# Splitting the first stage of a decoder block into a scale-only pass and a shift pass

## The chip, the cores and the metric

The kernel runs on one core of a Trainium2 chip. The metric is the device time of one execution in microseconds (us), and the reported number is the median of several executions. A profile is one further execution with the hardware profiler on; its own time is given apart. The engines are named as the profile names them: PE (TensorE, matrix products), DVE (VectorE, elementwise), ACT (ScalarE, activations and casts), POOL (GpSimd) and SP (SyncE, which in this kernel issues every transfer, in order, from one queue).

## The reference: what is computed

One block of a decoder with 512 tokens and width 2048, in float32. The parts that matter here:

```python
mod = silu(c) @ w_ada + b_ada                 # six rows of 2048: sh1, sc1, gt1, sh2, sc2, gt2
h = rmsnorm(x, norm1_g) * (1 + sc1) + sh1
p = h @ w_in                                  # 3360 recurrence columns, 1024 pooling columns
y_rwkv = rwkv7(token_shift_mix(p[:, :3360]))  # 16 heads of 64, recurrence over the tokens
u = p[:, 3360:]
mean = causal window mean of u (windows 2, 4, 8, 16, one per group of 256 columns)
y_pool = ((mean - u) @ pool_w + pool_b) * pool_scale
x = x + gt1 * (concat(y_rwkv, y_pool) @ w_out)
h = rmsnorm(x, norm2_g) * (1 + sc2) + sh2
x = x + gt2 * (silu(gate) * val of conv3(h @ w_up)) @ w_down
out = rmsnorm(x, norm_f_g)
```

The pooling branch takes a window mean minus the token itself. The term that sh1 adds to u is the same for every token, and a constant minus its own mean is zero. So the pooling columns can be computed without sh1, and the per-token factor of the first RMS norm can be put on after the product with w_in instead of ahead of it.

## The kernel before, in words

Activations lie transposed: features on the 128 partitions, the 512 tokens along the free axis. A width of 2048 is 16 slabs, called k. Every large product is made of three float32r products of split operands (hi·hi, hi·lo, lo·hi): `mm3`, lines 115 to 118. A weight block of 128x512 comes in by one 256 KB transfer (`wraw`, 4 buffers), ACT casts it to its hi half (L110, `whi`, 3 buffers) and DVE subtracts to get the lo half (L112, `wlo`, 3 buffers).

**First stage** (lines 171 to 223). All of x (4 MB) is loaded first; ACT squares it, DVE sums the squares, PE adds over partitions and broadcasts the RMS factor `rs`. Then a loop over the 16 k. For each k two rows of the adaLN product are made on DVE (L209: a 128x2048 block `wa` of 1 MB is multiplied by silu(c) and summed along the free axis), one for the scale sc1 (j = 16 + k), one for the shift sh1 (j = k). DVE forms `gsc` (L211) and `mod` (L213), then `modulate` makes the normalised input (L144 on DVE, L145 on ACT for the hi half, L146 on DVE for the lo half), and 24 products add slab k into eight PSUM banks `pf`: the first eight column tiles of w_in. The hi and lo halves of all 16 slabs stay in the slots `ah` and `al` (list H) for the later column tiles.

**Mixer stage** (lines 226 to 694). Four groups g = 0 to 3 of four heads each go through `front` and `rest`: a long chain over PE, ACT and DVE with two round trips through DRAM (`dn` and `nl`, then `dxy` and `X`) and a recurrence over 8 chunks. These steps have high priority in the scheduler that sets each engine's order. Below them, the other column tiles of w_in (48 products each, PSUM tag `mm`) are spread between them: 6 tiles of r, k and v in each of the first three groups, spilled to DRAM and read back by the next group. In the last group the 8 pooling tiles stand there (lines 672 to 680), each copied by ACT and spilled to DRAM (`su`). Four calls of `pool` (lines 274 to 300) then load a pair of them (`upad`, in the same memory as the tile k of the recurrence), do 1 to 4 window additions and a subtraction on DVE, two small products, and write the result to `mixd`. `load_pw` takes its memory from the tag `war`, which has two buffers. The same two buffers serve `ada_rest` (L341, L342): 96 rows of the remaining adaLN product, 512 KB each, 24 per group in program order, multiplied and summed on DVE. Because tags are handed out in program order, the last 24 of these rows can start only when the last `pool` calls have given their `war` buffers back.

**After that** comes the output product (`out_block`: 8 banks, four passes over four slabs, so 96 products per pass), which needs `mixd` read back (`mxl`, in the memory of `wraw`), then the MLP. From there on PE has work without a break to the end.

Of the kernel before, what the change touches and what calls it, by code (L numbers as in the profile page):

```python
# [59 lines left out]
def block_kernel(ctx, tc, a, out, stop=None, dbg=None):  # L60
# [113 lines left out]
    if True:  # L174
# [10 lines left out]
        with tc.tile_pool(name="ps00", bufs=1, space=PSUM) as ps00:
            pst = ps00.tile([P, NC], F32, tag="st", name="pst")
            acc = p0.tile([P, T], F32, tag="sacc", name="sacc")
            for k in range(KT):
                if k == 0:
                    S.activation(acc, xs[k], AF.Square)  # L190
                    continue
# [1 line left out]
                S.activation(sq, xs[k], AF.Square)
                V.tensor_add(acc, acc, sq)
            rms_stats(pst, acc)
            psb = ps00.tile([P, T], F32, tag="bc", name="psb")
            rms_bcast(psb, rms_rows(p0, pst, NC), NC)
            S.copy(rstd, psb)
        ps0ctx = ExitStack()
        ps0 = ps0ctx.enter_context(tc.tile_pool(name="ps0", bufs=1, space=PSUM))  # L200
        pf = [ps0.tile([P, T], F32, tag=f"pf{i}", name=f"pf{i}") for i in range(8)]
        H = []
        for k in range(KT):
            for part in (1, 0):
                j = part * 16 + k
                wa = p0.tile([P, D], F32, tag="wa", name="wa", bufs=4)
                nc.sync.dma_start(wa, a["ada1"][j, :, :])
                jk = p0.tile([P, D], BF16, tag="jk", name="jk", bufs=1)
                V.scalar_tensor_tensor(jk, wa, 1.0, cb, op0=ALU.mult, op1=ALU.mult,  # L209
                                       accum_out=mod[:, j : j + 1])  # L210
            V.scalar_tensor_tensor(gsc1[:, k : k + 1], mod[:, 16 + k : 17 + k], b1p[:, k : k + 1],  # L211
                                   col("n1", k), op0=ALU.add, op1=ALU.mult)
# [805 lines left out]
```

## Time and profile before

| what | value |
|---|---|
| median of 3 runs | 2406.44 us (2405.72 to 2408.11) |
| the profiled execution | 2404.25 us, span 2402.5 us |
| last product of the first stage starts | 153.53 us |
| start of the scores of group 3 | 573.3 us |
| end of the recurrence chain of group 3 (L646) | 666 us |
| the last of the 96 adaLN rows (L342) | 790 us |

Times in the views are microseconds from the start of the span; means of one instruction are nanoseconds. In the views of stretches, each engine has its busy time and, in brackets, its number of instructions; the last three numbers are the granted PE clock, the mean busy share of the DMA engines, and GB/s. PE's busy time counts overlapping products in full, so a busy PE is not a PE at its peak; the distance from one start to the next is what says how fast it goes.

### The profile page before, as it was taken

How to read it: one execution, taken by the hardware profiler on the slowest of the kernel's cores; microseconds unless marked ns; L12 is line 12 of the kernel's file. 1: busy time of each engine (PE TensorE's matmuls, PEld its weight loads, DVE VectorE, ACT ScalarE, POOL GpSimd, SP SyncE). 2: the span in 40 equal slices, each digit the busy share in tenths (PEclk: the TensorE clock that was granted, in tenths of full speed). 3: DMA queues.
4: the chain of work that ended last, by engine and by line, in shares of the span. 5: the costliest groups of instructions: out<-in, count | busy, mean ns of one | idle time of the engine just before them, and what ended most of it. 6: DMA issues, size and time to landing. Idle time of an engine off the chain costs nothing.

```text
span 2402.5 us, 36790 instructions
## 1 busy us (share of the span) xinstructions
PE 2247.2 (94%) x14434; PEld 1819.8 (76%) x14434; DVE 1338.7 (56%) x2208; ACT 815.5 (34%) x1339; POOL 27.2 (1%) x30
## 2 busy tenths in 40 slices
PE   4778898999988999999999999999999999999997
PEld 3656575676666799887888888888888888888887
DVE  7987786646446558568344434444344434444457
ACT  3242242434332346432233322332233323323333
POOL 0000000000000003000000000000000000000000
PEclk9989999999999999999999999999999999999999
DMA  9966767423257646357323333223322332333335
GB/s 360 342 207 198 232 215 221 135 85 107 75 170 249 221 158 203 122 186 253 99 98 97 97 96 97 97 97 97 97 97 97 97 97 97 96 98 97 98 99 175
DMA packets 182896, 351.79 MB, mean 146 GB/s; under 512 B 35905, under 2 KB 42305, under 8 KB 178497
## 3 DMA queue, kind: packets, MB, share of 16 engines
q1 hardware_dynamic: 182722, 349.44, 45.7%
q8 instruction: 113, 1.85, 0.3%
q14 instruction: 61, 0.50, 0.1%
HBM read 333.63 MB, written 15.74 MB: 145 GB/s over the span
## 4 chain that ended last, share of the span: by engine, by line
PE 71%; DMA 12%; DVE 11%; issue 3%; ACT 2%; SPq 1%; DVEq 0%; POOL 0%; ACTq 0%; POOLq 0%
PE b L116 21%; PE b L118 21%; PE b L117 21%; DMA war<-ada 5%; DVE jk L209 3%; PE mm L118 2%; PE mm L116 2%; PE mm L117 2%; DVE war L342 1%; DVE wlo L112 1%; DMA slot<-ada 1%; DMA wraw<-wup 1%; DMA wraw<-win 1%; DMA upad<-su 1%; DMA dxy<-xyl 0%
## 5 line engine op out<-in xcount | busy, mean ns | idle before, releaser
L110 ACT CAST whi<-wraw 128x512 fp32r<-128x512 f32 x788 | 489.1, 622 | 1253.4 <-PE b L117 959.6
L112 DVE TENSOR_TENSOR wlo<-wraw,whi 128x512 fp32r<-128x512 f32 x772 | 533.3, 692 | 665.8 <-ACT whi L110 657.4
L118 PE MATMUL b<-hh,wlo 128*128 128x512 f32 (+1 forms) x1472 | 561.1, 381 | 5.5 <-DVE wlo L112 4.1
L116 PE MATMUL b<-hh,whi 128*128 128x512 f32 (+1 forms) x1472 | 560.2, 381 | 0.0
L117 PE MATMUL b<-hl,whi 128*128 128x512 f32 (+1 forms) x1472 | 559.5, 380 | 0.0
L116 PE MATMUL b<-ah,whi 128*128 128x512 f32 (+1 forms) x1120 | 405.2, 362 | 15.7 <-ACT whi L110 12.8
L118 PE MATMUL b<-ah,wlo 128*128 128x512 f32 (+1 forms) x1120 | 403.8, 361 | 0.8 <-DVE wlo L112 0.8
L117 PE MATMUL b<-al,whi 128*128 128x512 f32 (+1 forms) x1120 | 403.4, 360 | 0.0
L118 PEld LDWEIGHTS b<-hh,wlo 128*128 128x128 f32 x1472 | 277.1, 188 | 61.2 <-DVE wlo L112 7.3
L116 PEld LDWEIGHTS b<-hh,whi 128*128 128x128 f32 x1472 | 277.2, 188 | 53.0 <-ACT whi L110 0.5
L117 PEld LDWEIGHTS b<-hl,whi 128*128 128x128 f32 x1472 | 277.1, 188 | 52.5
L116 PEld LDWEIGHTS b<-ah,whi 128*128 128x128 f32 x1120 | 212.5, 190 | 51.6 <-ACT whi L110 14.3
L118 PEld LDWEIGHTS b<-ah,wlo 128*128 128x128 f32 x1120 | 212.6, 190 | 33.5 <-DVE wlo L112 2.5
L117 PEld LDWEIGHTS b<-al,whi 128*128 128x128 f32 x1120 | 212.6, 190 | 32.6 <-DVE al L139 1.0
L118 PE MATMUL mm<-ah,wlo 128*128 128x512 f32 x432 | 179.3, 415 | 3.9 <-DVE wlo L112 3.9
L116 PE MATMUL mm<-ah,whi 128*128 128x512 f32 x432 | 178.3, 413 | 1.7 <-ACT whi L110 1.7
L117 PE MATMUL mm<-al,whi 128*128 128x512 f32 x432 | 176.5, 409 | 0.4 <-issue 0.4
L342 DVE SCALAR_TENSOR_TENSOR war<-war,cq 128x1024 f32<-128x1024 f32 x96 | 117.1, 1223 | 70.1 <-DMA war<-ada 69.5
L880 DVE SCALAR_TENSOR_TENSOR x<-b,mod,x 128x512 f32<-128x512 f32 x80 | 59.7, 751 | 111.7 <-PE b L118 111.7
L118 PEld LDWEIGHTS mm<-ah,wlo 128*128 128x128 f32 x432 | 83.0, 192 | 27.9 <-DVE wlo L112 6.9
L116 PEld LDWEIGHTS mm<-ah,whi 128*128 128x128 f32 x432 | 83.3, 193 | 23.5 <-issue 4.3
L117 PEld LDWEIGHTS mm<-al,whi 128*128 128x128 f32 x432 | 83.2, 193 | 20.2 <-issue 3.1
(220 smaller groups left out, 1708.7 us busy)
## 6 DMA issues: line engine op xcount, KB each, us to landing
wraw<-wup SPq DMA_DIRECT2D x368, 256.0 KB, 3.0
war<-ada SPq DMA_DIRECT2D x96, 512.0 KB, 4.3
wraw<-wdn SPq DMA_DIRECT2D x192, 256.0 KB, 2.7
wraw<-win SPq DMA_DIRECT2D x140, 256.0 KB, 4.0
wa<-ada SPq DMA_DIRECT2D x32, 1024.0 KB, 6.3
wraw<-wout SPq DMA_DIRECT2D x88, 256.0 KB, 3.4
slot<-ada SPq DMA_DIRECT2D x64, 256.0 KB, 3.7
sp<-spill SPq DMA_DIRECT2D x18, 256.0 KB, 2.3
```

What stands on the lines that cost most here:

```text
L110: S.copy(hi[:, 0:w], raw[:, 0:w])
L112: eng.tensor_tensor(lo[:, 0:w], raw[:, 0:w], hi[:, 0:w].bitcast(F32), op=ALU.subtract)
L116: PE.matmul(ps, wh, xh, start=start, stop=False)
L117: PE.matmul(ps, wh, xl, start=False, stop=False)
L118: return PE.matmul(ps, wl, xh, start=False, stop=stop)
L209: V.scalar_tensor_tensor(jk, wa, 1.0, cb, op0=ALU.mult, op1=ALU.mult, accum_out=mod[:, j : j + 1])
L342: V.scalar_tensor_tensor(wa, wa, 1.0, cq[0], op0=ALU.mult, op1=ALU.mult, accum_out=modq[:, kq, j : j + 1])
L880: V.scalar_tensor_tensor(x2[f], ps, mod[:, 80 + f : 81 + f], x2[f], op0=ALU.mult, op1=ALU.add)
```

## The change

The first stage becomes two passes over the 16 slabs.

*First pass.* Slab by slab, x is loaded (no longer all at first), the scale row of the adaLN product is made, and the raw x is multiplied by `gsc` alone (hi on ACT, lo on DVE, into the slots `ah` and `al`). These are multiplied with seven of the eight pooling tiles, in seven PSUM banks (21 products per slab). The squares for the RMS factor are summed alongside. After the pass, the eighth bank serves for the RMS statistics and its broadcast, then for the eighth pooling tile, a full product of 48 with all 16 slabs. Each of the eight tiles is multiplied by `rs` on DVE and spilled to `su` (256 KB each, two buffers `us`).

*Second pass.* Slab by slab the shift row is made, the full normalised input is formed as before in the same slots, and the eight column tiles that were the first stage's before are computed in all eight banks.

The eight pooling tiles of the last group are gone from the mixer stage; `pool` reads `su` as it did. The input arrays on the host are laid out to fit (`winu`, `winu7`). Weights are read as often as before.

```diff
-        xs = []
-        for i in range(8):
-            xt = p0.tile([P, 2, T], F32, tag=f"x{i}", name=f"x{i}")
-            nc.sync.dma_start(xt, a["xT"][:, 2 * i : 2 * i + 2, :])
...
+        pu = [pf_bank(i) for i in range(7)]
+        xs, H1 = [], []
+        acc = p0.tile([P, T], F32, tag="sacc", name="sacc")
+        for k in range(KT):
+            if k % 2 == 0:
+                xt = p0.tile([P, 2, T], F32, tag=f"x{k // 2}", name=f"x{k // 2}")
+                nc.sync.dma_start(xt, a["xT"][:, k : k + 2, :])
+                xs += [xt[:, 0, :], xt[:, 1, :]]
+            ada_row(16 + k)
+            V.scalar_tensor_tensor(gsc1[:, k : k + 1], mod[:, 16 + k : 17 + k], b1p[:, k : k + 1],
+                                   col("n1", k), op0=ALU.add, op1=ALU.mult)
+            hi, lo = slots(k)
+            S.activation(hi, xs[k], AF.Copy, scale=gsc1[:, k : k + 1])
+            V.scalar_tensor_tensor(lo, xs[k], gsc1[:, k : k + 1], hi[:, :].bitcast(F32), op0=ALU.mult, op1=ALU.subtract)
+            H1.append((hi, lo))
+            feed(pu, a["winu"], k, H1[k])
...
+                S.activation(sq, xs[k], AF.Square)
+                V.tensor_add(acc, acc, sq)
+        pst = pf_bank(7)
+        rms_stats(pst, acc)
...
+        S.copy(rstd, psb)
+        pu.append(pf_bank(7))
+        project(pu[7], a["winu7"], H1)
+        for i in range(8):
+            t = p0.tile([P, T], F32, tag="us", name="us", bufs=2)
+            V.tensor_mul(t, pu[i], rstd)
+            d = tc.dram_tile([P, T], F32, name=f"su{i}")
+            nc.sync.dma_start(d, t)
+            su[POOLS[i // 2], i % 2] = d
+        pf = [pf_bank(i) for i in range(8)]
         H = []
         for k in range(KT):
-            for part in (1, 0):
-                j = part * 16 + k
...
+            ada_row(k)
             V.tensor_add(mod[:, k : k + 1], mod[:, k : k + 1], col("b_ada", k))
             h = p0.tile([P, T], F32, tag="h", name="h", bufs=2)
             hi, lo = slots(k)
             modulate(hi[:, :], lo[:, :], h, xs[k], rstd, gsc1[:, k : k + 1], mod[:, k : k + 1])
...
+            feed(pf, a["win0"], k, H[k])
...
-        else:
-            for n, gi in enumerate(POOLS):
-                for i in range(2):
-                    ps = win_tile(27 + 2 * n + i)
-                    t = ra.tile([P, T], F32, tag="spill", name="spill", bufs=2)
-                    S.copy(t, ps)
-                    d = tc.dram_tile([P, T], F32, name=f"su{gi}_{i}")
-                    nc.sync.dma_start(d, t)
-                    su[gi, i] = d
```

Three places in the order of the engines' instructions show what moves.

First stage, DVE, one slab. Names: `jk` is an adaLN row (L209 before, L191 after), `wlo` a weight's lo half, `sacc` the sum of squares, `al` the lo half of the input. Before, one slab of the loop:

```order
L209 SCALAR_TENSOR_TENSOR jk,mod<-wa,cb 128x2048
L211 SCALAR_TENSOR_TENSOR gsc_86<-mod,b1p,vec 128x1
L144 SCALAR_TENSOR_TENSOR h<-x_120,gsc_86,rs_132 128x512
L209 SCALAR_TENSOR_TENSOR jk,mod<-wa,cb 128x2048
L112 TENSOR_TENSOR wlo<-wraw,whi 128x512
L213 TENSOR_TENSOR mod<-mod,vec 128x1
L112 TENSOR_TENSOR wlo<-wraw,whi 128x512
L146 SCALAR_TENSOR_TENSOR al_431<-h,mod,ah_430 128x512
```

The change, two slabs of the first pass:

```order
L191 SCALAR_TENSOR_TENSOR jk,mod<-wa,cb 128x2048
L112 TENSOR_TENSOR wlo<-wraw,whi 128x512
L211 SCALAR_TENSOR_TENSOR gsc_86<-mod,b1p,vec 128x1
L112 TENSOR_TENSOR wlo<-wraw,whi 128x384
L223 TENSOR_TENSOR sacc<-sacc,sq 128x512
L215 SCALAR_TENSOR_TENSOR al_271<-x_218,gsc_86,ah_270 128x512
L223 TENSOR_TENSOR sacc<-sacc,sq 128x512
L191 SCALAR_TENSOR_TENSOR jk,mod<-wa,cb 128x2048
L112 TENSOR_TENSOR wlo<-wraw,whi 128x512
L211 SCALAR_TENSOR_TENSOR gsc_86<-mod,b1p,vec 128x1
L112 TENSOR_TENSOR wlo<-wraw,whi 128x384
L215 SCALAR_TENSOR_TENSOR al_318<-x_310,gsc_86,ah_317 128x512
```

A slab has one `jk` row instead of two, and the sum of squares has moved into the loop.

Group 3, DVE, from the two solve steps X and Y into the first chunks of the recurrence. Names: `sall` and `rc` belong to the recurrence, `sw` and `z` to `pool`, `war` is a row of `ada_rest`. Before (L555 X, L561 Y):

```order
L555 TENSOR_TENSOR X<-X,bt 128x1024
L284 TENSOR_TENSOR sw<-sw 128x2x513
L561 TENSOR_TENSOR Y<-Y,bt 128x1024
L289 SCALAR_TENSOR_TENSOR z<-sw,upad 128x1024
L547 TENSOR_TENSOR pm<-bt,mlev 128x1024
L290 TENSOR_TENSOR z<-sw,prec 128x2x16
L112 TENSOR_TENSOR wlo<-wraw,whi 128x512
L291 TENSOR_TENSOR z<-z,upad 128x2x16
L278 MEMSET upad 128x2x16
L561 TENSOR_TENSOR Y<-Y,bt 128x1024
L604 TENSOR_SCALAR sall<-ch,fdec 128x64 x2
L112 TENSOR_TENSOR wlo<-wraw,whi 128x512
```

The change (L580 X, L586 Y, L367 the adaLN row):

```order
L580 TENSOR_TENSOR X<-X,bt 128x1024
L367 SCALAR_TENSOR_TENSOR war,modq<-war,cq 128x1024
L586 TENSOR_TENSOR Y<-Y,bt 128x1024
L572 TENSOR_TENSOR pm<-bt,mlev 128x1024
L367 SCALAR_TENSOR_TENSOR war,modq<-war,cq 128x1024
L586 TENSOR_TENSOR Y<-Y,bt 128x1024
L367 SCALAR_TENSOR_TENSOR war,modq<-war,cq 128x1024
L629 TENSOR_SCALAR sall<-ch,fdec 128x64 x2
L605 TENSOR_TENSOR rc<-ch,xv 128x128
L367 SCALAR_TENSOR_TENSOR war,modq<-war,cq 128x1024
L627 SCALAR_TENSOR_TENSOR sall<-ch,fdec,sf 128x64 x2
L605 TENSOR_TENSOR rc<-ch,xv 128x128
```

All four `pool` calls now stand ahead of X, and the last 24 adaLN rows, which stood behind the whole chain, stand between its steps: 13 of them ahead of the sum that closes the recurrence (`y`, L648 after, L623 before), 18 ahead of its last step (L671 after, L646 before).

Group 3, SP, the same rows' transfers. Before:

```order
L299 DMA mixd_105<-mxp 128x512
L341 DMA war<-ada 128x1024
L299 DMA mixd_106<-mxp 128x512
L280 DMA upad<-su_1_5930 128x512
L341 DMA war<-ada 128x1024 x2
L299 DMA mixd_101<-mxp 128x512
```

The change (L366 the adaLN row, L324 a result of `pool`, L108 a weight block, L723 a read of `mixd`):

```order
L324 DMA mixd_105<-mxp 128x512
L366 DMA war<-ada 128x1024
L324 DMA mixd_106<-mxp 128x512
L366 DMA war<-ada 128x1024
L324 DMA mixd_101<-mxp 128x512
L366 DMA war<-ada 128x1024 x2
L324 DMA mixd_102<-mxp 128x512
L366 DMA war<-ada 128x1024 x19
L108 DMA wraw<-wout 128x512
L366 DMA war<-ada 128x1024
L723 DMA mxl<-mixd_97 128x512
```

No weight block stands between these rows any more; before, a weight block or a read of `mixd` stood behind nearly every one of them.

More of the change, by code (lines that the diff above doesn't have):

```diff
@@ L51 @@
     WIN_ORDER += [f"r{_p}", f"k{_p}", f"v{_p}"]
-WIN_ORDER += [f"u{2 * _g + _i}" for _g in POOLS for _i in range(2)]
+POOL_ORDER = [f"u{2 * _g + _i}" for _g in POOLS for _i in range(2)]
 MIX_ORDER = [0, 1, 2, 3, 4, 5] + [8 + 2 * _g + _i for _g in POOLS for _i in range(2)] + [6, 7]
@@ L178, in block_kernel @@
         nc.sync.dma_start(cact, cb[0:1, :])
-        xs = []
-        for i in range(8):
-            xt = p0.tile([P, 2, T], F32, tag=f"x{i}", name=f"x{i}")
-            nc.sync.dma_start(xt, a["xT"][:, 2 * i : 2 * i + 2, :])
-            xs += [xt[:, 0, :], xt[:, 1, :]]
-        rstd = p0.tile([P, T], F32, tag="rs0", name="rs0")
[L185 to L191, printed above, removed]
+        su = {}
@@ new lines, in block_kernel, with pf_bank, ada_row @@
+        rstd = p0.tile([P, T], F32, tag="rs0", name="rs0")
+        ps0ctx = ExitStack()
+        ps0 = ps0ctx.enter_context(tc.tile_pool(name="ps0", bufs=1, space=PSUM))
+        def pf_bank(i):
+            return ps0.tile([P, T], F32, tag=f"pf{i}", name=f"pf{i}")
+        def ada_row(j):
+            wa = p0.tile([P, D], F32, tag="wa", name="wa", bufs=4)
+            nc.sync.dma_start(wa, a["ada1"][j, :, :])
+            jk = p0.tile([P, D], BF16, tag="jk", name="jk", bufs=1)
+            V.scalar_tensor_tensor(jk, wa, 1.0, cb, op0=ALU.mult, op1=ALU.mult, accum_out=mod[:, j : j + 1])
@@ new lines, in feed @@
+        def feed(banks, src, k, hl):
+            n = len(banks)
+            for i0 in range(0, n, WC // P):
+                m = min(WC // P, n - i0)
+                wh, wl = split_weights(src[k, :, i0 * P : (i0 + m) * P])
+                for ii in range(m):
+                    sl = slice(ii * P, (ii + 1) * P)
+                    mm3(banks[i0 + ii], wh[:, sl], wl[:, sl], *hl, start=k == 0, stop=k == KT - 1)
+        pu = [pf_bank(i) for i in range(7)]
+        xs, H1 = [], []
+        acc = p0.tile([P, T], F32, tag="sacc", name="sacc")
@@ L194, in block_kernel @@
                 V.tensor_add(acc, acc, sq)
[L195 to L201, printed above, removed]
+        pst = pf_bank(7)
+        rms_stats(pst, acc)
+        dg = rms_rows(p0, pst, NC)
+        psb = pf_bank(7)
+        rms_bcast(psb, dg, NC)
+        S.copy(rstd, psb)
[8 more added lines that the diff above has]
+        pf = [pf_bank(i) for i in range(8)]
         H = []
         for k in range(KT):
-            for part in (1, 0):
-                j = part * 16 + k
[L206 to L212, printed above, removed]
+            ada_row(k)
             V.tensor_add(mod[:, k : k + 1], mod[:, k : k + 1], col("b_ada", k))
```

17 lines of the change are left out of this document (9 added, 8 removed).

## Prediction

> **What bounds the kernel now.** I read the page's slices first, then a table of stretches by stage, then the timeline inside the two stages that the change touches.
>
> ```profile
> PE   4778898999988999999999999999999999999997
> DVE  7987786646446558568344434444344434444457
> ...
> 154.00:301.00 147.00, 119.66 (x1527) 86.83 (x1528) 108.16 (x199) 52.05 (x88) 1.91 (x2) 0.93 0.66 207
> 301.00:448.00 147.00, 131.48 (x1574) 94.86 (x1573) 106.20 (x193) 52.49 (x87) 0.95 (x1) 0.95 0.65 207
> 448.00:552.00 104.00, 98.50 (x1467) 71.36 (x1466) 60.53 (x112) 43.12 (x73) 0.96 (x1) 1.00 0.31 90
> 552.00:666.00 114.00, 104.95 (x1489) 77.98 (x1488) 65.17 (x118) 41.85 (x71) 0.00 (x0) 0.99 0.32 96
> 666.00:800.00 134.00, 111.48 (x431) 82.28 (x430) 72.17 (x115) 36.53 (x59) 0.00 (x0) 0.91 0.73 234
> 800.00:2403.00 1603.00, 1578.71 (x7561) 1328.41 (x7559) 793.67 (x1286) 540.55 (x889) 21.01 (x16) 0.99 0.38 118
> ```
>
> From 800 us on PE is busy for 98.5% and nothing there is changed: whatever the change is worth arises before 800 us, and it is simply how much earlier or later PE arrives at that point. The stretch 154 to 552 us holds groups 0 to 2, with the same instructions before and after. So two places decide: the first stage (to 154 us), and group 3 with what follows it (552 to 800 us).
>
> In the first stage DVE sets the pace.
>
> ```profile
> L209 DVE SCALAR_TENSOR_TENSOR jk<-wa,cb 128x2048 bf16<-128x2048 f32 x32 | 73.1, 2285 | 0.0
> L112 DVE TENSOR_TENSOR wlo<-wraw,whi 128x512 fp32r<-128x512 f32 x33 | 22.4, 687 | 0.6 <-ACT whi L110 0.6
> L146 DVE SCALAR_TENSOR_TENSOR al<-h,mod,ah 128x512 fp32r<-128x512 f32 x16 | 12.0, 752 | 2.5 <-ACT ah L145 2.5
> L194 DVE TENSOR_TENSOR sacc<-sacc,sq 128x512 f32<-128x512 f32 x15 | 10.4, 692 | 9.5 <-ACT sq L193 8.1
> ...
> 60.00:80.00 20.00, 15.84 (x60) 11.93 (x60) 19.30 (x28) 4.94 (x8) 0.00 (x0) 0.91 0.95 334
> ...
> 63.71 1.19 PE L116 MATMUL pf<-ah,whi 128*128 128x512 f32 x4 [1.91 <-ACT ah L145]
> 64.36 2.28 DVE L209 SCALAR_TENSOR_TENSOR jk<-wa,cb 128x2048 bf16<-128x2048 f32 x1
> 66.45 0.63 PE L118 MATMUL pf<-ah,wlo 128*128 128x512 f32 x1
> 66.88 0.63 PE L117 MATMUL pf<-al,whi 128*128 128x512 f32 x1
> 69.09 0.40 PE L117 MATMUL pf<-al,whi 128*128 128x512 f32 x1
> 69.32 0.39 PE L118 MATMUL pf<-ah,wlo 128*128 128x512 f32 x1
> 72.03 2.28 DVE L209 SCALAR_TENSOR_TENSOR jk<-wa,cb 128x2048 bf16<-128x2048 f32 x1
> ```
>
> One slab takes 72.03 - 64.36 = 7.67 us, and DVE works 19.30 of 20 us. A product follows the last one after 0.227 us at full clock (69.09 to 69.32, 0.227 over longer runs), so PE needs only 24 x 0.227 = 5.4 us of a slab. Some spells run at 0.43 us (66.45 to 66.88): the clock is then halved.
>
> **First stage, new.** *First pass.* DVE per slab: one `jk` row 2.3 with its read-out 0.1, `gsc` 0.2, a whole and a three-quarter `wlo` 0.69 + 0.52, `sacc` 0.69, `al` 0.75: 5.25 us. Neighbours overlap by some 0.05 us (the old list adds up to 8.0 for a 7.67 us slab), so 4.95, but `al` follows `gsc` with only a `wlo` between and waits for ACT's hi half, about half a microsecond in every second slab. PE needs 21 x 0.227 = 4.8, the transfers 1.79 MB at the 334 GB/s of the row above 5.3. Three engines stand within 10%, so I take 5.4 us (bounds: 4.95 for DVE alone; 6.0 if the transfers fall to 300 GB/s).
>
> ```profile
> 9.11 1.91 ACT L177 ACTIVATE cb<-cb 128x2048 f32<-128x2048 f32 x1 [7.10 <-DMA cb<-c]
> ...
> 153.53 0.39 PE L118 MATMUL pf<-ah,wlo 128*128 128x512 f32 x1
> ```
>
> silu(c) is done at 11.0, two squares on ACT and one `sacc` go first, so the first row starts near 13; 16 x 5.4 brings DVE to 99.5 and PE to 103. The statistics stand on PE ahead of the last two slabs and cost nothing there.
>
> *Between the passes.* The eighth tile is 48 x 0.227 = 10.9 us of PE. Beside it DVE has to empty eight banks (0.75 each, by L146's row) through two buffers `us`; each pair waits for the transfers of the pair before it, queued on SP behind weight blocks. I count a pair per 4.5 us: the first near 106, the last near 122, while PE wants the last two banks at 120. That is 2 us of stall.
>
> *Second pass.* PE needs 384 x 0.227 = 87 us; DVE needs 5.1 per slab against 5.44, and has some three rows in hand. I add 3 us. So the last product starts near 115 + 87 + 5 = 207 instead of 153.5: **+53 us**. Bounds: +42 (4.95 per slab, no stall), +71 (6.0 in both passes, which is also PE at the granted 0.91 of the 60 to 80 us row).
>
> **Groups 0 to 2.** Before the first scan of group 0, DVE now has 11 `ada_rest` rows instead of 4, which fill slack at the end of the second pass. The group without such rows took 104 us, those with them 147 each: 86 us for 72 rows, 1.2 each. Seven fewer, half of them only moved: **-3 us** (0 to -8).
>
> **Group 3.** By the order, some 33 of the 384 pooling products stood ahead of the scores; the others lay between and behind the steps of this chain:
>
> ```profile
> 589.23 0.29 DVE L513 COPY xyl<-nl 128x256 f32<-128x256 f32 x1 [3.37 <-DMA nl<-dn]
> ...
> 598.60 0.38 DVE L523 COPY xyl<-xyl 128x256 f32<-128x256 f32 x1
> ...
> 611.87 1.26 DVE L284 TENSOR_TENSOR sw<-upad 128x1054 f32<-128x1054 f32 x1 [5.16 <-DMA upad<-su]
> 613.05 1.22 DVE L547 TENSOR_TENSOR pm<-bt,mlev 128x1024 f32<-128x1024 f32 x1
> ...
> 617.10 1.21 DVE L555 TENSOR_TENSOR X<-X,bt 128x1024 f32<-128x1024 f32 x1
> ...
> 625.03 1.22 DVE L561 TENSOR_TENSOR Y<-Y,bt 128x1024 f32<-128x1024 f32 x1 [1.22 <-PE bt L559]
> ...
> 652.90 1.22 DVE L623 TENSOR_TENSOR y<-y,bt 128x1024 f32<-128x1024 f32 x1 [2.03 <-PE bt L622]
> ...
> 665.64 1.22 DVE L646 TENSOR_TENSOR rs<-rs,bt 128x1024 f32<-128x1024 f32 x1
> ...
> 719.72 1.23 DVE L342 SCALAR_TENSOR_TENSOR war<-war,cq 128x1024 f32<-128x1024 f32 x1 [7.03 <-DMA war<-ada]
> 724.61 1.23 DVE L342 SCALAR_TENSOR_TENSOR war<-war,cq 128x1024 f32<-128x1024 f32 x1 [0.66 <-DMA war<-ada]
> 784.84 1.23 DVE L342 SCALAR_TENSOR_TENSOR war<-war,cq 128x1024 f32<-128x1024 f32 x1 [0.57 <-DMA war<-ada]
> 787.21 1.23 DVE L342 SCALAR_TENSOR_TENSOR war<-war,cq 128x1024 f32<-128x1024 f32 x1 [0.39 <-DMA war<-ada]
> DMA to landing us min/median/max: 3.4/4.1/5.5
> ```
>
> I follow the new order in old times (as if the first stage had not moved). Up to 589 nothing changes: the dn/nl round trip is the wait. Into the solve (589.2 to 598.6) go the rest of the first pool and the second, some six operations of 1.15 us, and 1.8 us of `wlo` leave: +5, `xyl` at 604. The third pool fits into the second round trip; the fourth needs its own load behind the eight X transfers on SP, so `pm` falls to 617 (+4), X to 621.
>
> From there the 24 `war` rows stand in DVE's queue between the steps, and whatever stands behind one waits for its transfer. While the fourth pool holds the other buffer, one row takes a whole cycle (719.72 to 724.61: 4.9 us): rows at 622, 627, 632, which puts Y at 629 (+4). Then two buffers serve: 3.4 to 4.1 to land and 1.3 on DVE, shared by two, make 2.4 to 2.7 us a row (784.84 to 787.21 shows 2.4), and I take 2.6. Thirteen rows before y, the fourth at 636: 636 + 9 x 2.6 = 660, y at 661 (+8); without them the emptied chain would be there near 652. The 18th row is at 674 and L646 at 676 instead of 666, the last row at 690 instead of 790.
>
> The output product starts behind it. Three weight blocks are ready, so 36 products run to 680; the next `wlo` stands behind row 21 (683), two more behind rows 22 and 23, and the blocks of the second pass behind the last row on SP. I get the second pass of 96 products at 699, the third at 720, then without break.
>
> ```profile
> 666.00:800.00 134.00, 52.64 (x191) 35.57 (x189) 0.00 (x0) 8.54 (x12) 0.91 0.73 234
> ...
> 720.00:740.00 20.00, 9.74 (x43) 8.07 (x44) 0.00 (x0) 0.00 (x0) 0.81 0.57 175
> 740.00:760.00 20.00, 19.22 (x84) 15.29 (x83) 0.00 (x0) 0.00 (x0) 1.00 0.90 291
> 760.00:780.00 20.00, 16.02 (x69) 12.21 (x67) 0.00 (x0) 0.00 (x0) 0.97 0.86 273
> 780.00:800.00 20.00, 13.85 (x48) 11.13 (x49) 0.00 (x0) 0.00 (x0) 0.69 0.99 344
> ```
>
> The first row is for the tag mm (pooling tiles and the products of `pool`), the others for the output products before: 43 + 84 + 69 + 48 = 244 by 800. The new order has 244 at 720 + 52 x 0.227 = 732: -68 us. Against it, an emptied PE loses its clock: the 0.43 spell above ran for seven products, 1.4 us, after an idle of 1.9 us; with some three such gaps on the path I take 4 us back. **-64 us** (-20 if rows keep the one-buffer cycle, -78 if none of them delays a step).
>
> The Trainium skill, "TensorE: Matmul & The Clock Gate", Part 1, says that PE falls to half its clock after an idle window of about 3.4 us and needs as long to recover; the halved spacing above agrees, though its gap was shorter. By that rule alone, every wait of group 3 would leave PE cold, and the sum would lose perhaps 8 us instead of 4.
>
> **Sum.** +53 - 3 - 64 = -14 us, 2404.25 - 14 = 2390 for the profiled execution. The median stands 2.2 us above that one: **2392 us**.
>
> **The rivals.** *A, slower:* the rows stay at the one-buffer cycle. Place: DVE between X and the end of group 3. From the fourth row 20 more intervals at 4.9 instead of 2.6 cost 46 us: 2438. The sign turns where a row costs 2.6 + 14/20 = 3.3 us, and the earlier 3.4 to 5.5 us landings are not far from that; against it, two buffers gave 2.4 even with weight blocks between. *B, no change or slightly slower:* the passes run at 6 us a slab, since DVE, PE and transfers all stand near full: +18, 2410. For it speaks the DMA share of 0.95 at 334 GB/s. *C, a larger gain:* the rows land in time, the chain without foreign products runs faster than before: -78 instead of -64, 2378. *D, the removed products were only in gaps:* group 3 ends as before and only the last adaLN rows move; removing them is worth 30 us, the sum +20, 2426. Against it: after 666 us, where no chain was left, PE still had 191 less at most 32 of `pool`, so 160 of these products, to do: 36 us.
>
> **How the numbers follow.** Forecast 0.55 (own range 2376 to 2407), A 0.10, B 0.17, C 0.13, D 0.05. Less than 0.2%, 4.8 us, cannot be told from no change. Faster: most of the forecast (0.48), C, and a little of B: 0.64. Same: 0.05 of the forecast and 0.07 of B: 0.13 with rounding. Slower: A, D and the rest: 0.23. The range of eight in ten reaches over C and B and into D: 2364 to 2426.
>
> **What would show it.** Right: `jk` rows 5.2 to 5.7 us apart in the first pass, PE near full in the second, its last product near 207 us; in group 3 DVE idle with releaser "war<-ada" between `sall` steps, rows 2.4 to 2.8 us apart, the last one 45 to 50 us earlier than before, no stretch of output products under 70 per 20 us but the first. Wrong: slabs near 6 us, a stall of over 8 us between the passes, rows near 4.9 us apart to the end, or a chain of group 3 that ends no later than 110 us after its scores but with output products that still trickle.

## The result, and the profile after

The changed kernel takes 2392.97 us (median of 6 runs, 2389.72 to 2400.24); the kernel before, run beside it, 2407.03 us (6 runs, 2403.63 to 2408.14). The ratio is 0.9945, 95% interval 0.993 to 0.9961. The forecast was 2392 us. The profiled execution took 2392.89 us, with a span of 2391.0 us instead of 2402.5.

From the page of the changed kernel, the span in 40 slices of 59.8 us, and below it stretches by stage (busy time and number of instructions of PE, weight loads, DVE, ACT, POOL; then granted clock, DMA share, GB/s):

```profile
PE   7998889899668999999999999999999999999997
DVE  7897778664755458567344433444344434444457
PEclk9998999999879999999999999999999999999999
```

```profile
0.00:206.00 206.00, 183.85 (x778) 147.39 (x778) 169.50 (x258) 77.56 (x127) 2.36 (x10) 0.99 0.86 308
206.00:605.00 399.00, 349.61 (x4564) 252.20 (x4564) 270.33 (x494) 148.13 (x246) 3.82 (x4) 0.96 0.55 169
605.00:720.00 115.00, 72.21 (x1283) 48.96 (x1281) 78.71 (x142) 33.05 (x56) 0.00 (x0) 0.78 0.50 152
720.00:800.00 80.00, 72.68 (x293) 56.63 (x294) 40.42 (x65) 25.76 (x41) 0.00 (x0) 0.94 0.69 223
800.00:2391.00 1591.00, 1567.75 (x7521) 1319.66 (x7519) 789.79 (x1281) 536.83 (x883) 21.37 (x16) 1.00 0.38 117
```

The weak slices have moved. Before, PE was thin at the very start (slices 1 to 3) and dipped again from 660 to 780 us; now the start is fuller, and the hole lies at 600 to 720 us, where group 3's chain stands alone (72 of 115 us busy, clock 0.78). Groups 0 to 2 have the same 4564 PE instructions and the same length, 399 us here and 398 before.

The first stage in the timeline of the changed kernel (start, duration, engine, line, operation; in brackets the idle time before and what ended it):

```profile
44.37 2.28 DVE L191 SCALAR_TENSOR_TENSOR jk<-wa,cb 128x2048 bf16<-128x2048 f32 x1
54.14 2.28 DVE L191 SCALAR_TENSOR_TENSOR jk<-wa,cb 128x2048 bf16<-128x2048 f32 x1
86.85 2.28 DVE L191 SCALAR_TENSOR_TENSOR jk<-wa,cb 128x2048 bf16<-128x2048 f32 x1
88.20 1.28 ACT L157 ACT_TABLE_LOAD   x1 [2.54 <-PE pf L152]
90.42 3.30 PE L116 MATMUL pf<-ah,whi 128*128 128x512 f32 x7 [2.30 <-ACT ah L214]
96.12 0.56 DVE L112 TENSOR_TENSOR wlo<-wraw,whi 128x384 fp32r<-128x384 f32 x1 [2.57 <-ACT whi L110]
101.70 1.02 PE L165 MATMUL pf<-rdiag,cmat 128*128 128x512 f32 x2
103.39 0.50 PE L116 MATMUL pf<-ah,whi 128*128 128x512 f32 x1 [0.67 <-ACT rs L229]
120.28 0.50 PE L116 MATMUL pf<-ah,whi 128*128 128x512 f32 x1 [0.98 <-DVE us L234]
205.78 0.39 PE L118 MATMUL pf<-ah,wlo 128*128 128x512 f32 x1
```

Two slabs of the first pass take 54.14 - 44.37 = 9.77 us, 4.88 each. At its end the statistics hold PE up: ACT loads a table and takes the square root ahead of the hi half that the next slab needs, PE waits 2.30 us and then does seven products at half clock, and DVE waits 2.57 us for a weight half. The last product of the stage starts at 205.78 us; before it was 153.53.

Group 3 in the timeline of the changed kernel:

```profile
605.59 2.33 DVE L415 TENSOR_TENSOR_SCAN sg<-scanm,sg 128x1040 f32<-128x1040 bf16 x1
627.13 3.26 PE L465 MATMUL bt<-ar,inv 64*64 64x128 f32 x64 [7.63 <-DVE inv L456]
633.34 1.26 DVE L309 TENSOR_TENSOR sw<-upad 128x1054 f32<-128x1054 f32 x1 [0.96 <-DMA upad<-su]
645.33 0.28 DVE L538 COPY xyl<-nl 128x256 f32<-128x256 f32 x1
677.04 1.22 DVE L580 TENSOR_TENSOR X<-X,bt 128x1024 f32<-128x1024 f32 x1 [0.20 <-issue]
679.29 1.23 DVE L367 SCALAR_TENSOR_TENSOR war<-war,cq 128x1024 f32<-128x1024 f32 x1 [1.02 <-DMA war<-ada]
684.24 1.23 DVE L367 SCALAR_TENSOR_TENSOR war<-war,cq 128x1024 f32<-128x1024 f32 x1 [1.45 <-DMA war<-ada]
689.06 1.23 DVE L367 SCALAR_TENSOR_TENSOR war<-war,cq 128x1024 f32<-128x1024 f32 x1 [2.45 <-DMA war<-ada]
694.52 1.22 DVE L367 SCALAR_TENSOR_TENSOR war<-war,cq 128x1024 f32<-128x1024 f32 x1 [3.00 <-DMA war<-ada]
718.62 1.22 DVE L648 TENSOR_TENSOR y<-y,bt 128x1024 f32<-128x1024 f32 x1
722.17 1.22 DVE L367 SCALAR_TENSOR_TENSOR war<-war,cq 128x1024 f32<-128x1024 f32 x1 [1.19 <-DMA war<-ada]
732.88 1.21 DVE L671 TENSOR_TENSOR rs<-rs,bt 128x1024 f32<-128x1024 f32 x1
```

The chain from the scan to its end (L671) takes 127.3 us; before it took 665.64 - 552.53 = 113.1. The first rows are 4.9, 4.8 and 5.5 us apart, and then eleven intervals from 694.52 to 722.17 make 2.5 us each. The output products in stretches of 20 us:

```profile
720.00:740.00 20.00, 9.09 (x38) 7.05 (x38) 0.00 (x0) 0.00 (x0) 0.89 0.64 191
740.00:760.00 20.00, 18.58 (x72) 14.93 (x73) 0.00 (x0) 0.00 (x0) 0.85 0.70 223
760.00:780.00 20.00, 19.43 (x85) 15.47 (x84) 0.00 (x0) 0.00 (x0) 1.00 0.89 318
780.00:800.00 20.00, 20.00 (x90) 16.40 (x89) 0.00 (x0) 0.00 (x0) 1.00 0.52 159
```

38 + 72 + 85 are done by 780 us, 49 more of the last 90 make 244 near 791; before, 244 were done at 800. Nine of the 11.5 us by which the profiled span is shorter are there at that point.

### The profile page after: what moved, and what is told of

Read it like the earlier page. It is cut to its first block, busy times and chain, and to the rows that moved or that the text cites. A ratio compares the mean times of both kernels' runs of the same rounds, so it can differ in the third digit from the quotient of the medians.

```text
span 2391.0 us, 36818 instructions
## 1 busy us (share of the span) xinstructions
PE 2246.1 (94%) x14434; PEld 1824.8 (76%) x14434; DVE 1348.8 (56%) x2236; ACT 821.3 (34%) x1351; POOL 27.5 (1%) x30
## 4 chain that ended last, share of the span: by engine, by line
PE 74%; DMA 11%; DVE 10%; issue 3%; ACT 1%; SPq 1%; DVEq 0%; POOL 0%; ACTq 0%; POOLq 0%
PE b L116 21%; PE b L118 21%; PE b L117 21%; DMA war<-ada 5%; PE pf L116 2%; PE pf L117 1%; DVE war L367 1%; PE pf L118 1%; DVE wlo L112 1%; DMA slot<-ada 1%; PE mm L118 1%; PE mm L116 1%; PE mm L117 1%; DMA wa<-ada 1%; DVE slot L858 1%
## 5 line engine op out<-in xcount | busy, mean ns | idle before, releaser
L112 DVE TENSOR_TENSOR wlo<-wraw,whi 128x512 fp32r<-128x512 f32 (+1 forms) x776 | 533.7, 689 | 651.3 <-ACT whi L110 645.6
L110 ACT CAST whi<-wraw 128x512 fp32r<-128x512 f32 (+1 forms) x792 | 488.8, 619 | 1185.3 <-PE b L117 956.3
L117 PEld LDWEIGHTS b<-hl,whi 128*128 128x128 f32 x1472 | 277.2, 188 | 52.3
L116 PEld LDWEIGHTS b<-ah,whi 128*128 128x128 f32 x1120 | 212.0, 189 | 37.8 <-ACT whi L110 3.9
L117 PEld LDWEIGHTS b<-al,whi 128*128 128x128 f32 x1120 | 212.0, 189 | 32.4 <-DVE al L139 1.2
L367 DVE SCALAR_TENSOR_TENSOR war<-war,cq 128x1024 f32<-128x1024 f32 x96 | 117.0, 1222 | 64.3 <-DMA war<-ada 63.7
L118 PE MATMUL mm<-ah,wlo 128*128 128x512 f32 x304 | 126.8, 417 | 3.7 <-DVE wlo L112 3.7
L116 PE MATMUL mm<-ah,whi 128*128 128x512 f32 x304 | 127.1, 418 | 1.5 <-ACT whi L110 1.5
L117 PE MATMUL mm<-al,whi 128*128 128x512 f32 x304 | 125.0, 411 | 0.7 <-issue 0.7
L116 PE MATMUL pf<-ah,whi 128*128 128x512 f32 x256 | 96.1, 405 | 20.2 <-ACT ah L214 18.5
L118 PE MATMUL pf<-ah,wlo 128*128 128x512 f32 x256 | 101.2, 396 | 2.0 <-DVE wlo L112 1.9
L117 PE MATMUL pf<-al,whi 128*128 128x512 f32 x256 | 101.0, 395 | 0.0
```

Source lines behind the costliest of these rows:

```text
L110: S.copy(hi[:, 0:w], raw[:, 0:w])
L112: eng.tensor_tensor(lo[:, 0:w], raw[:, 0:w], hi[:, 0:w].bitcast(F32), op=ALU.subtract)
L116: PE.matmul(ps, wh, xh, start=start, stop=False)
L117: PE.matmul(ps, wh, xl, start=False, stop=False)
L118: return PE.matmul(ps, wl, xh, start=False, stop=stop)
L367: V.scalar_tensor_tensor(wa, wa, 1.0, cq[0], op0=ALU.mult, op1=ALU.mult, accum_out=modq[:, kq, j : j + 1])
```

## The experiments

Milestones of every kernel, read from its timeline (us from the start of the span; "244th" is the start of the 244th output product), and its ratio to the kernel before, which ran on the same chip in the same sitting:

| kernel | last product of first stage | scan of group 0 | scan of group 3 | end of chain 3 | 244th | ratio (95%) |
|---|---|---|---|---|---|---|
| before | 153.5 | 171.9 | 552.5 | 665.6 | 800.7 | 1 |
| changed | 205.8 | 224.7 | 605.6 | 732.9 | 791.5 | 0.9945 (0.993 to 0.9961) |
| b_nopool | 153.9 | 172.6 | 556.6 | 680.9 | 739.1 | 0.9732 (0.9708 to 0.9755) |
| b_rowsfree | 153.1 | 172.1 | 580.0 | 683.0 | 792.4 | 0.9986 (0.9975 to 0.9996) |
| a_rowsfree | 203.5 | 223.1 | 630.5 | 745.5 | 802.0 | 0.9979 (0.9966 to 0.9991) |
| a_late24 | 202.5 | 222.0 | 603.7 | 722.0 | 779.6 | 0.9932 (0.9912 to 0.9953) |
| a_late24b | 204.3 | 224.9 | 605.0 | 725.8 | 784.0 | 0.9945 (0.9931 to 0.996) |
| a_seven | 200.8 | 220.7 | 603.1 | 733.0 | 790.7 | 0.9933 (0.9916 to 0.9951) |
| a_four | 181.2 | 201.3 | 585.2 | 712.7 | 776.2 | 0.9901 (0.9886 to 0.9917) |
| a_four_late | 180.9 | 200.6 | 587.2 | 708.0 | 772.6 | 0.9902 (0.9884 to 0.9921) |
| a_sq | 212.0 | 231.8 | 609.4 | 739.0 | 797.8 | 1.0025 (1.0012 to 1.0039) |
| a_four_sq | 177.0 | 196.9 | 589.4 | 716.7 | 783.4 | 0.9913 (0.9893 to 0.9934) |
| a_four_half | 182.0 | 200.9 | 582.5 | 725.2 | 785.1 | 0.9927 (0.9914 to 0.994) |
| a_four_sq_half | 177.4 | 196.0 | 579.0 | 722.3 | 783.4 | 0.9918 (0.9903 to 0.9932) |

The theory is the prediction's: the first stage pays 53 us for the 384 products; group 3 gains 64, since they no longer stand behind its chain and the last adaLN rows move up. The rivals that the runs below bear on: the products were only in gaps and the rows' position is what counts (D), rows between the steps cost nothing (C), or they cost much more (A).

**Group 3 alone (b_nopool).** In the kernel before:

```diff
-                    ps = win_tile(27 + 2 * n + i)
...
-                    su[gi, i] = d
+                    su[gi, i] = sp[2 + n // 2, 2 * (n % 2) if i else 1]
```

> The kernel before, but the 384 products of the eight pooling tiles are left out of the last group (that part of the computation is missing: the pool reads other spilled tiles of the same size, and the first stage is the old one). The change's gain in group 3 by itself. Theory (the foreign products and the wait of the last adaLN rows for the pool's buffers cost group 3 64 us in all): 2407 - 64 = 2343 us; in the trace the group-3 chain is some 10 to 14 us longer from its scan to its end than in the kernel before, rows 2.4 to 2.8 us apart, the last row some 95 us earlier from the scan on. Rival (the products only filled gaps of PE, and what counts is that the last rows move): 2407 - 30 = 2377 us.

Measured: 2339.0 us beside 2404.3, -65 (-59 to -70 by the interval). The chain takes 124.3 us from its scan, 11 longer than before, and the 244th product comes 182.5 us after the scan instead of 248.2. Theory: -64; rival D, which had 30 us for taking the products out, is out. What the changed kernel has on top of this is its first stage, 0.9945 - 0.9732 = 2.1% or 51 us, and its trace has 205.8 - 153.9 = 51.9. So the two halves of the change add up.

**The last adaLN rows freed (b_rowsfree, a_rowsfree).** One line, in the kernel before and in the changed one:

```diff
-        t = ra.tile([P, 2 * T], F32, tag="war", name="pw", bufs=2)
+        t = cell("R", "pw")
```

> The kernel before with one line changed: the pool's weights lie in the memory of r, which is dead by then, and no longer in the two buffers of the adaLN rows. So the last 24 rows can start before the pool and move into groups 1 and 2; nothing else changes. Theory (a row in a group without slack costs about 1 us: groups 0 and 1 took 277 us with 72 rows where two groups without rows take 207): +24 us in the groups; after the end of the chain some 160 pooling products and 244 output products run without a row between them, 404 x 0.227 = 92 us instead of 134, -42 us: 2407 - 18 = 2389 us. Rival (only the position of the last rows made the change's gain in group 3, and rows cost nothing where PE has work): 2407 - 42 = 2365 us, better than the changed kernel without its first stage.

> The changed kernel with the same one line: the pool's weights in the memory of r, so that the last 24 rows leave the recurrence of group 3 and move into groups 1 and 2. Theory (a row costs about 1 us in a group that PE fills, and the 24 rows between the steps of group 3's chain cost it some 8 to 14 us): +24 - 12 = +12, 2405 us. Rival (rows cost nothing in groups 1 and 2, which have PE work to cover them): 2393 - 12 = 2381 us.

Measured: 2401.0 us, -3 instead of -18, and 2399.7 us, about 8 above the changed kernel (the theory had +12). In both the rows go into groups 1 and 2: in the kernel before, 4 more in group 1 and 20 in group 2, in the changed kernel 12 more in each. Group 2 is longer for it: it takes 127.5 us with 20 rows in it and 103.2 without, 1.2 us a row if all of it is put down to the rows. The rows and the group as a whole, first in the kernel before with freed rows, in the stretch of its group 2 (the tag of the rows on DVE, then all engines):

```profile
452.00:580.00 128.00, 24.49 (x40) 0.95 0.52 167
...
452.00:580.00 128.00, 117.63 (x1527) 86.84 (x1526) 86.17 (x162) 46.42 (x78) 0.95 (x1) 0.95 0.52 167
```

and the same group of the kernel before:

```profile
449.30:552.50 103.20, 97.70 (x1464) 70.69 (x1463) 59.73 (x111) 42.32 (x72) 0.96 (x1) 1.00 0.31 91
```

The rows' own 24.5 us of DVE is about what the group grows by, but that doesn't make it the cause. PE has 63 instructions more in the longer group (1527 and 1464), an estimate of 14 us at 0.227 each, and group 3 has that work less. So 1.2 us is the most that a row can have cost there; no run separates the two. From the scan of group 3 to the 244th product 36 us come back in the one kernel (212.4 instead of 248.2) and 14 in the other (171.5 instead of 185.9), 12 of them within the chain. Moving the rows gains in group 3, then, and is paid for in the groups ahead of it: -3 us in all.

**Rows out of the mixer (a_late24, a_late24b).** The rows feed only the second norm, so they can wait. The first kernel has one half row behind every block of the output products, the second puts them behind the reload of x:

```diff
-            wa = ra.tile([P, 2 * T], F32, tag="war", name="war", bufs=2)
...
+            t = rb.tile([P, T], F32, tag=f"hh{i}" if i < 16 else f"hl{i - 16}", name="wl")
+            nc.sync.dma_start(t, a["ada2"][kq, j, :, h * T : (h + 1) * T])
+            V.scalar_tensor_tensor(t, t, 1.0, csl[kq, h], op0=ALU.mult, op1=ALU.mult,
...
             out_block(f, k0)
+            ada_late(1)
```

> The changed kernel with the last 24 adaLN rows moved out of the mixer, behind the start of the output products (as 48 half rows, through memory that is free until the second norm; they feed only the second norm's scale and part of its shift). Group 3's chain has no row left in it, groups 0 to 2 keep theirs. Theory of the prediction (rows between the steps delay the chain by 8 of its 10 us, and DVE has room beside the output products): the chain ends 8 to 14 us earlier, 2393 - 10 = 2383 us. Rival 1 (the chain is held by the pool's operations and its own waits, not by rows): chain and total unchanged, 2393 us. Rival 2 (the rows beside the output products make weight halves late): output products under 80 per 20 us, 2395 to 2405 us.

> The changed kernel with the last 24 adaLN rows moved out of the mixer as before, but later: behind the reload of x, in the last pass of the output products and the tiles after it. The first version lost some 35 products of 0.227 us between 740 and 820 us to rows whose transfers came late, while 4 MB of x and 3.7 MB of mixed input were loaded too. Theory: that loss (8 us) goes, chain as in the first version (118 us from scan to end instead of 127): 2382 us. Rival (the rows make weight halves late wherever they stand): 2388 us.

Measured: 2388.6 and 2391.7 us, both within the interval of the changed kernel. The chain does end earlier, after 118.3 and 120.9 us instead of 127.3: the rows had cost it 6.4 to 9 us, as the theory says. The rest of its excess over the 113.1 of before, 5 to 8 us, isn't theirs. But the output products pay some or all of it back. From the scan to the start of the last of them it is 302.0 us in the first kernel and 308.3 in the second, beside 309.5 in the changed one: the first keeps 7.5 us of its 9 (in a profiled execution that is the fastest of its four), the second 1.2 of its 6.4. In stretches of 20 us, the first kernel and then the second:

```profile
740.00:760.00 20.00, 18.63 (x75) 13.80 (x76) 0.00 (x0) 0.00 (x0) 1.00 0.81 272
760.00:780.00 20.00, 18.15 (x75) 13.45 (x74) 0.00 (x0) 0.00 (x0) 1.00 0.88 288
```

```profile
760.00:780.00 20.00, 18.59 (x78) 13.75 (x76) 0.00 (x0) 0.00 (x0) 1.00 0.83 280
780.00:800.00 20.00, 17.14 (x73) 13.28 (x72) 0.00 (x0) 0.00 (x0) 1.00 0.80 268
```

73 to 78 products where 85 to 90 fit. DVE, which works in order, stands before half rows that haven't landed for 16.8 us between 720 and 780 us in the first kernel and for 19.4 between 740 and 800 in the second, and the weight half behind them is late; at 0.8 of DMA share this happens with or without the reload of x. What rival 2 of the first kernel said of the products was right, its time of 2395 to 2405 us wasn't: 2388.6 lies between the theory's 2383 and rival 1's 2393, and the medians can't tell either late kernel from the changed one.

**The eighth tile (a_seven).** Seven tiles in the first pass, the eighth back in group 3, `us` with seven buffers:

```diff
-        project(pu[7], a["winu7"], H1)
-        for i in range(8):
-            t = p0.tile([P, T], F32, tag="us", name="us", bufs=2)
+        for i in range(NU):
+            t = p0.tile([P, T], F32, tag="us", name="us", bufs=NU)
```

> The changed kernel, but the eighth pooling tile is not computed between the passes; its 48 products go back to group 3, and the buffers `us` are seven, so that the seven banks are emptied without waiting for their spills. Theory (PE is the bound of the first stage and idle in group 3's chain): 10.9 us of products and 2 us of waits for banks leave the first stage, but the chain statistics, broadcast, emptying of seven banks (4.5 us), first modulate (2 us), which the eighth tile covered, is then bare, about 8 us from the last product of pass 1 to the first of pass 2: the last product of the stage 5 us earlier, group 3 as long as in the changed kernel, 2386 us. Rival (the 48 products delay group 3's chain as much as they save): 2391 us.

Measured: the last product of the stage 4.9 us earlier, where 5 was worked out. Without the tile the path from the last product over statistics, emptied banks and first `modulate` lies bare:

```profile
109.72 2.93 PE L116 MATMUL pf<-ah,whi 128*128 128x512 f32 x6 [6.40 <-ACT ah L145]
```

So the eighth tile is half paid for by what it covers. Of the 4.9 us, 2.5 are left at the scan of group 3 and 0.8 at the 244th product; 2389.8 us can't be told from the changed kernel.

**Four tiles (a_four), the version that beats both.** As above with `NU = 4`; the tiles of the last two pools stay in group 3.

> The changed kernel with four of the eight pooling tiles in the first pass and four in group 3 (those of the last two pools). First pass: PE has 12 products a slab, 2.7 us; if PE set the pace of 4.88 us a slab, the slab falls to DVE's 4.3 us (row 2.28 and read-out, gsc 0.13, sum 0.61, al 0.67, one weight half 0.6); if the transfers set it (1.79 MB a slab), 1.54 MB come at 4.2 us; if something else does, it stays at 4.9. Four banks are free for the statistics, no eighth tile: the last product of the stage some 22 us earlier than in the changed kernel. Group 3: 192 products run in the idle time of PE beside the chain (in the kernel before, 224 of 384 were done by the chain's end); the last adaLN rows start behind the third pool and run beside the output products. Theory: -22 for the stage, +10 for rows between output products, 2379 us. Rival (any foreign product in group 3 costs its full 0.227 us): -22 + 44 = 2413 us.

Measured: 2380.7 us, ratio 0.9901; its interval ends at 0.9917, below the 0.993 at which that of the changed kernel begins. The first stage ends 24.6 us earlier (22 worked out), though the slab hardly shrinks: it takes 4.75 us, two rows being 9.49 us apart (59.54 to 69.03), where 4.2 to 4.3 was worked out for PE's 12 products. In group 3 the chain takes 127.4 us, as long as with no tile there. That pair alone doesn't show that the tiles are free, since 18 of the last 24 rows now run behind the chain and not 6. The kernels without any row in group 3 compare better: 120.8 us with four tiles (a_four_late, below), 118.3 and 120.9 with none (a_late24, a_late24b), so the tiles cost the chain 2.5 us at most. From the scan to the 244th product, with the 18 rows beside the output products, a_four takes 191.0 us and the changed kernel 185.9: 5.1 us, where the theory had 10. Stretches of group 3 in this kernel, and in the changed one at the same distance from the scan:

```profile
605.00:625.00 20.00, 17.16 (x359) 13.39 (x358) 17.60 (x23) 6.18 (x9) 0.00 (x0) 1.00 0.34 96
625.00:645.00 20.00, 20.00 (x92) 16.24 (x90) 13.00 (x41) 5.23 (x10) 0.00 (x0) 1.00 0.52 156
645.00:665.00 20.00, 17.40 (x478) 11.89 (x476) 12.20 (x14) 5.37 (x8) 0.00 (x0) 1.00 0.40 137
```

```profile
625.00:645.00 20.00, 12.54 (x324) 10.43 (x324) 13.61 (x14) 4.55 (x5) 0.00 (x0) 0.71 0.24 60
645.00:665.00 20.00, 9.57 (x19) 3.97 (x20) 16.07 (x47) 3.11 (x4) 0.00 (x0) 0.80 0.41 116
665.00:685.00 20.00, 15.91 (x419) 10.75 (x420) 12.12 (x16) 3.35 (x4) 0.00 (x0) 0.86 0.51 149
```

With products between the steps PE is busy 17 to 20 of 20 us at full clock; emptied, it is busy 10 to 16 at a clock of 0.71 to 0.86, and the chain is no shorter. At the 244th product a_four is 15.3 us ahead of the changed kernel, in the span 11.6, in the medians beside each other 0.44% or 10.6 us.

**Four tiles with late rows (a_four_late).** Both edits together.

> The kernel with four pooling tiles in the first pass, and the last 24 adaLN rows moved out of the mixer into the second half of the output products (48 half rows in memory that is free until the second norm), behind the reload of x. Theory (the rows cost 8 to 14 us where they stand in or behind group 3, and nothing beside output products once the transfers have room, DVE having 8 of 20 us busy there): 10 us less than the kernel with four tiles and rows in the mixer, 2369 us, output products 85 to 90 per 20 us throughout. Rival (rows are covered where they were): no difference.

Measured: 2380.9 us, no difference from a_four. The chain is 6.6 us shorter (120.8), and again the output products give it back: at the last of them 0.7 us of it is left.

**The sum of squares on PE (a_sq, a_four_sq).**

```diff
-                V.tensor_add(acc, acc, sq)
-        pst = pf_bank(7)
-        rms_stats(pst, acc)
+            for i in range(NC):
+                PE.matmul(pst[:, i : i + 1], sq[:, i * P : (i + 1) * P], ones[:, 0:1],
+                          start=k == 0 and i == 0, stop=k == KT - 1 and i == NC - 1)
```

> The changed kernel with the sum of squares taken off DVE: PE adds the squares of each slab over partitions (four products of one column, accumulated over the 16 slabs) instead of DVE adding the slabs first. DVE has 0.61 to 0.69 us less per slab of the first pass. Theory A (DVE sets the pace of 4.88 us a slab, PE with 21 x 0.227 = 4.77 and the transfers stand just behind): the slab can fall only to 4.8 plus the four small products (0.16 to 0.25 us each, partly overlapped), no gain in pass 1; the statistics at the end wait less on DVE: 0 to -3 us, 2389 us. Theory B (the four small products add up on PE): slab 5.3, +7, 2398 us.

> The kernel with four pooling tiles in the first pass, and the sum of squares taken off DVE in the same way. Its slab took 4.75 us with PE at 57 products per 20 us, though its 12 products need 2.7 us. Theory (DVE sets that pace: row, weight half, gsc, wait of 0.79 us for ACT's hi half in every second slab, lo half, sums): the slab falls by 0.4 to 0.6 us to 4.2, 16 slabs give -8 us: 2373 us, the last product of the stage near 173 instead of 181. Rival (the transfers set it: DMA share 1.02 at 408 to 416 GB/s from 20 to 60 us): the slab stays at 4.7, 2381 us.

Measured with seven tiles: 2408.7 us, slower than before. DVE falls from 19.35 to 15.1 of 20 us, PE has not an idle moment, and the slab rises to 5.72 us (rows at 46.76 and 58.20, two slabs apart). The first pass with the squares on PE:

```profile
40.00:60.00 20.00, 20.00 (x105) 16.99 (x104) 15.11 (x20) 7.75 (x14) 0.00 (x0) 1.00 0.86 307
...
40.71 0.95 PE L221 MATMUL pf<-cmat,sq 128*128 128x1 f32 x8
41.52 1.19 PE L116 MATMUL pf<-ah,whi 128*128 128x512 f32 x4
```

So PE stood directly behind DVE (21 x 0.227 = 4.77 of 4.88 us), and 0.81 us of small products a slab go straight onto it: theory B, with a slab above its 5.3. The profiled execution, the fastest of the 12, is 6.2 us above the changed kernel's span, all of it in the first stage; why the median lies 9.6 us above this execution no trace shows.

Measured with four tiles: the slab falls from 4.75 to 4.49 us, DVE to 16.8 of 20 us, and DVE now waits 0.79 us in every slab for ACT's hi half. That wait, not the transfers, is what is left, so the rival is out; the stage ends 4.2 us earlier instead of 8. At the scan of group 3 the gain is gone: groups 0 to 2 take 392.5 us instead of 383.9, in an order that the scheduler made anew. 2382.6 us, no difference from a_four.

**Rows in halves (a_four_half, a_four_sq_half).**

```diff
-            wa = ra.tile([P, 2 * T], F32, tag="war", name="war", bufs=2)
-            nc.sync.dma_start(wa, a["ada2"][kq, j, :, :])
+            for h in range(2):
...
+                wa = ra.tile([P, T], F32, tag="war", name="war", bufs=4)
+                nc.sync.dma_start(wa, a["ada2"][kq, j, :, hs])
```

> The kernel with four pooling tiles in the first pass, and all 96 adaLN rows cut into two halves of 256 KB with four buffers instead of two of 512 KB, in the same memory; the sums are put together at the end. In the changed kernel DVE waits 58 us for rows between 215 and 760 us. Theory (what a row costs a group is DVE standing in order before a row that hasn't landed; halves land sooner and four are under way): half of those waits go, groups 0 to 2 take some 20 us less, 2361 us. Rival (a row's price is its own work on DVE and the queue of transfers; 192 halves of 0.69 + 0.08 us cost 25 us more DVE time than 96 rows of 1.22 + 0.08): groups 0 to 10 us longer, 2381 to 2390 us.

> Four pooling tiles in the first pass with both edits: sum of squares on PE, adaLN rows in halves with four buffers. The two act in different places (first stage, mixer groups), so theory: the sum of their two effects, 2381 - 8 - 20 = 2353 us. Rival (each only uncovers the next bound): the better one alone, 2361 us or above.

Measured: 2386.9 and 2383.2 us; neither gains. From 200 to 590 us, around groups 0 to 2, first with whole rows, then with halves:

```profile
L366 DVE SCALAR_TENSOR_TENSOR war<-war,cq 128x1024 f32<-128x1024 f32 x66 | 80.5, 1223 | 44.9 <-DMA war<-ada 44.1 <-DVE war L366 0.4
```

```profile
L368 DVE SCALAR_TENSOR_TENSOR war<-war,cq 128x512 f32<-128x512 f32 x131 | 87.6, 688 | 37.5 <-DMA war<-ada 36.5 <-DVE spill L255 0.7
```

The idle time ahead of the rows falls by 7 us, their work rises by 7 (and by 5 more for twice as many read-outs), and the groups are 2 us shorter. The chain of group 3 takes 142.7 us; 31 half rows now stand ahead of its end, where a_four has 6 whole rows. Half of the waits were to go and a sixth went, so finer pieces of the same transfers weren't waited for much less, and whether the wait is what a row costs stays open.

## Why the prediction was right, point by point

- *"+53" for the first stage:* +52.3 at the last product, and +51 as the difference of two timed kernels. Inside it two steps were off and nearly cancel. "I take 5.4 us" a slab: 4.88, the bound that was given for DVE alone. I had put a margin on three engines within 10% of each other; they overlap fully (DVE 19.35, PE 88 products, DMA share 0.94 to 0.98). a_sq and a_four_sq show the order: DVE first, PE 2% behind it, the transfers third. Against that, "the statistics cost nothing there" was wrong: the sixteenth row starts at 86.85 us, 7 us ahead of the 94 that 5.4 us a slab would give, but PE is done with the pass only when the broadcast (L165) starts at 101.70, 1.3 us ahead of the 103 worked out. The table load and the square root are in ACT's queue ahead of the hi half of the next slab; that was the wait to look for. That the first stage came out within 1 us is luck in this respect.
- *"2 us of stall" between the passes:* the eighth tile starts at 103.39 (103 worked out), the first wait for a bank is 0.98 us at 120.28; the pairs of `us` stand where they were put. a_seven shows what the tile hid: 6.4 us of idle PE.
- *"-3" for groups 0 to 2:* +0.3. From the scan of group 0 to that of group 3 it was 380.6 us and is 380.9, though 61 rows stand there instead of 68. The step that failed: the rows that run before the first scan (11 instead of 4) were counted as saved at a mean price of 1.2 us, taken from the length of groups with and without rows. By the prediction's own stretches those with rows also hold 60 and 107 PE instructions more (1527 and 1574 beside 1467), by an estimate up to 38 of the 86 us at 0.227 each. Seven rows fewer beside the same PE work (4533 instructions from scan to scan in both kernels) saved nothing that shows. b_nopool, with 68 rows, took 384.1 us there, so a difference of 3 us is no clear sign either way.
- *"-64" for group 3:* the 244th product comes 62.3 us earlier from the scan on, and the rest of the span is 2.3 us shorter, together -64.6. The rows came as read: 4.8 to 5.5 us apart while the pool held a buffer, then 2.5 (2.6 predicted); the last one runs at 748.0 us, 42 us earlier than before, where 45 to 50 was predicted. The chain was 14.2 us longer where 10 was worked out. The step that failed is "up to 589 nothing changes": the copy from `nl` comes 3.0 us later. The pool's first addition now stands between the two score steps on DVE (`sb`, L467) and waits 0.96 us for its load (633.34), and the two halves of `al` (L505), of which one stood between these steps before, go ahead of both. PE idles 7.63 us before the scores; what that adds isn't shown by itself. All later points carry these 3 to 4 us: `X` at 677.0 where 674 would follow, y at 718.6 and not 714, the end at 732.9 and not 729. The 4 us taken back for the clock stood for three spells of 1.4 us; the granted clock is 0.78 over the whole of 605 to 720 us, and what that costs in all no run shows. That -64.6 meets -64 is in part luck, since the 2.3 us behind the 244th product were not forecast.
- *"those rows delay the chain":* shown by taking them out, from 127.3 to 118.3 and 120.9 us. The prediction had y at 661 with rows and 652 without.
- *Rival C (rows delay nothing, the emptied chain is faster):* half of it is wrong by those 6 to 9 us; against the other half, the emptied chain without rows is still longer than before, with a lower clock (last section). *Rival A:* no, 2.5 us a row. *Rival B:* no, 4.88 us a slab. *Rival D:* b_nopool gains 65 us where D had 30.
- *The sum:* in the profiled executions it is -11.5 us where -14 was forecast; the medians of six runs differ by 14.1. That 2392 and 2392.97 agree to 1 us is therefore luck in part.
- *What wasn't seen:* the split. The argument that 160 products remained after the chain said at the same time that 224 were free inside it. Moving only what didn't fit was the better change, by about 10 us.

## What to carry to other kernels

Before work is moved out of a latency-bound stage, count how much of it that stage hides, and move only the rest: here four of eight tiles cost some 5 us where they were, up to the 244th product, and their absence shortens the first stage by 24.6. This stage, in which three engines stand within a few per cent, ran at the largest of them, not above it, but an edit that unloads one must not load the next (0.8 us a slab put on PE cost more than the 0.65 us taken from DVE gave). And an early finish of one stage isn't always banked: of 4.9 (a_seven) and 4.2 us (a_four_sq) gained in the first stage, less than one arrived 600 us later, in orders that the scheduler had made anew.
